# Reciprocal roots as a power on GpSimd, decay exponents in the bias of ScalarE's exponential, and one last convolution tap

## The chip, the core and the metric

The kernel runs on one core of a Trainium2 chip. The metric is device microseconds of one execution. The trace is one execution taken by the hardware profiler; its times are microseconds (us) unless marked ns. The five engines appear in it as PE (TensorE matmuls; PEld is its weight load), DVE (VectorE), ACT (ScalarE), POOL (GpSimd) and SP (SyncE, which only issues DMAs here). Each engine works through its own queue in order and waits for the others through semaphores.

## The reference

One inference step of a trunk of two layers, in float32, for a prompt of 512 tokens and 8 samples of one token that share the weights. Layer 0 mixes tokens by a gated MLP with spatial mixing in chunks of 128, layer 1 by a gated DeltaNet; each is followed by a SwiGLU part, and a norm ends the trunk. What bears on the change:

```python
def rmsnorm(x, g):
    xf = xf * lax.rsqrt(jnp.mean(xf * xf, axis=-1, keepdims=True) + EPS)

def l2norm(x):
    return xf * lax.rsqrt(jnp.sum(xf * xf, axis=-1, keepdims=True) + EPS)

# short convolution of 4 taps over q, k and v, samples from their own state
for j in range(1, CONV_W):
    y = y + full[:, j:j + T] * w[j]

# gated delta rule, in chunks
beta = jax.nn.sigmoid(b_raw)
gc = jnp.cumsum(g, axis=-1)
decay = jnp.where(incl, jnp.exp(gc_i - gc_j), 0.0)
L = jnp.where(strict, (k * beta) @ k.T * decay, 0.0)
Tm = inverse of (I + L)
A = (q @ k.T) * decay
```

The last block is shortened; the outputs are the activations of prompt and samples and the new states.

## The kernel before

The 520 columns (512 of the prompt, 8 of the samples) are kept features first and are worked in two halves of 256 and 264 columns. Each weight tile (128 output features, 512 KB) is loaded by SP's queue (L130), cast on ScalarE into a high part (L138) and subtracted into a low part (L139), on VectorE or, for some tiles, on GpSimd: in the delta layer the first 17 of the tiles in `order` (`POOL_LO`), and elsewhere the last two of an output projection. A half tile is then 24 matmuls, three per 128 input features (`products`, L168), so a tile is 48. `stream` splits a weight tile one ahead of its use. A scheduler orders each engine's instructions by the order of the program and by readiness; the transposes and norm matmuls inside `pin` keep their place among the matmuls. `after(n, step)` emits a step behind the n-th half tile from now.

**Roots.** `rsqrt` (L107 to L124) computes 1/sqrt by an integer guess and two polynomial steps: nine VectorE operations (L114 to L123) on 3 to 64 columns. It is called 34 times: ten times for the norms, eight for the keys, and for the spatial gate, the queries, the samples and the outputs of the scan. For a norm, TensorE sums squares over partitions (L205, L207), VectorE scales the sum (L208), `rsqrt` follows, VectorE puts the factor on a diagonal (L221), TensorE spreads it (L227), ScalarE copies it to SBUF (L230), and VectorE applies it to each product (L238).

**Keys.** The key stage is `key_tile` for eight heads. `conv_tile` (L568) multiplies two half products by the norm (L574), scales them by the first tap on ScalarE (L577), adds three taps on VectorE over 512 columns (L579) and a fourth operation for the eight columns of the samples (L580), and ends with a Silu on ScalarE (L581). Two half tiles later `normalise` transposes the key on TensorE (L618), squares it four times on ScalarE with an accumulated sum (L621), adds eps (L622), takes the root and scales on VectorE (L624). Four half tiles after the convolution `back` transposes again (L629). With the first four heads, `decay` loads rows by DMA, masks them on GpSimd (L558) and subtracts the cumulated decay on VectorE (L559); with heads 2 and 4 an Exp over 16 chunks at once follows on ScalarE (L654). `lower` multiplies key by key on TensorE (L643) and applies beta and decay in four VectorE operations per head (L645).

**Behind the keys.** The inverse of I + L is a chain of VectorE operations (L670 to L689) beside gate tiles; its blocks are merged with TensorE while `decay` and `query_conv` prepare the queries, with two more Exps of 16 chunks (L753). Then come the value tiles and the scan (`scan_step`), whose outputs take a root too (L832 to L836). The kernel ends with the last norm: L208, the root, then the scaling of the tokens out of PSUM (L1010 on ScalarE, L1012 on VectorE) and the stores.

Of the kernel before, what the change touches and what calls it, by code (L numbers as in the profile page):

```python
# [15 lines left out]
P = 128  # L16
# [22 lines left out]
def trunk(  # L39
# [55 lines left out]
    G.memset(ones, 1.0)  # L95
    warm = cst.tile([P, 1], F32, name="warm")
# [9 lines left out]
    # ---------------------------------------------------------------- helpers  # L106
    def rsqrt(s, n, p=P):  # L107
        if n <= 32:
            y = sm.tile([P, 32], F32, tag="rs_y", name=nm("rs_y"), bufs=4)[:p, :n]
            u = sm.tile([P, 32], F32, tag="rs_u", name=nm("rs_u"))[:p, :n]  # L110
        else:
            y, u = t1()[:p, :n], t1()[:p, :n]
        yi = y.bitcast(I32)
        V.tensor_scalar(yi, s.bitcast(I32), 1, None, ALU.logical_shift_right)  # L114
        V.tensor_scalar(yi, yi, -1, 0x5F1FFFF9, ALU.mult, ALU.add)
        # a Newton step with balanced error, scaled by 3/8, then one of third order
        V.scalar_tensor_tensor(u, y, -0.375 * 0.703952253, y, ALU.mult, ALU.mult)
        V.tensor_tensor(u, u, s, ALU.mult)  # L118
        V.scalar_tensor_tensor(y, u, 0.375 * 0.703952253 * 2.38924456, y, ALU.add, ALU.mult)
        V.scalar_tensor_tensor(u, y, 64.0 / 9.0, y, ALU.mult, ALU.mult)  # L120
        V.tensor_tensor(u, u, s, ALU.mult)
        V.scalar_tensor_tensor(u, u, -10.0 / 3.0, u, ALU.add, ALU.mult)
        V.scalar_tensor_tensor(y, u, 5.0, y, ALU.add, ALU.mult)  # L123
        return y  # L124
# [23 lines left out]
    def after(n, step):  # L148
        """Emit a step behind the n-th half tile of products from now."""
        steps.setdefault(done[0] + n, []).append(step)  # L150
# [26 lines left out]
    class Norm:  # L177
        """RMSNorm whose per-token factor is applied after the products."""
# [19 lines left out]
        def factors(self, h):  # L198
            c0, n = HALF[h]
            ps = axps()  # L200
            s = small([P, 3], "nrm_s")
            G.memset(s, 1.0)
            for i, (o, w) in enumerate(PARTS[h]):
                rest = self.rest.get(h)
                pin(PE.matmul(ps[:w, i:i + 1], lhsT=self.acc[:, c0 + o:c0 + o + w], rhs=ones[:, 0:1], start=True, stop=rest is None))  # L205
                if rest is not None:
                    pin(PE.matmul(ps[:w, i:i + 1], lhsT=rest[:, o:o + w], rhs=ones[:, 0:1], start=False, stop=True))  # L207
            V.tensor_scalar(s[:, 0:2], ps[:, 0:2], 1.0 / D, EPS, ALU.mult, ALU.add)  # L208
            if h:
                V.tensor_scalar(s[:NS, 2:3], ps[:NS, 2:3], 1.0 / D, EPS, ALU.mult, ALU.add)  # L210
            return rsqrt(s, 3)
# [29 lines left out]
    class Feed:  # L241
        """Takes finished tiles of x: parts of x * gain for the products, squares for the norm."""
# [43 lines left out]
    # the tensor engine's clock rises while the first loads run  # L286
# [4 lines left out]
    # ---------------------------------------------------------------- input  # L291
# [23 lines left out]
    # ---------------------------------------------------------------- layer 0: spatial gating  # L315
# [51 lines left out]
    V.tensor_scalar(sv, sv, 1.0 / DA, EPS, ALU.mult, ALU.add)  # L367
# [14 lines left out]
    V.tensor_scalar(svs, ps[:, :NS], 1.0 / DA, EPS, ALU.mult, ALU.add)  # L382
# [34 lines left out]
    # ---------------------------------------------------------------- swiglu  # L417
# [38 lines left out]
    # ---------------------------------------------------------------- layer 1: gated delta net  # L456
# [7 lines left out]
    # conv contributions of the sample states  # L464
# [28 lines left out]
    # beta and decay, columns in (head, chunk) order, the samples as a fifth chunk  # L493
# [26 lines left out]
    V.tensor_scalar(beta, beta, 1.0, None, ALU.add)  # L520
    V.reciprocal(beta, beta)
    V.scalar_tensor_tensor(sp, ax, 0.0, sp, ALU.max, ALU.add)
# [7 lines left out]
    V.tensor_copy(gc, ps[:, 0:32])  # L530
    egl = cst.tile([P, H, NCH], F32, name="egl")
# [12 lines left out]
    # samples: decay and the factors of the prediction  # L544
# [9 lines left out]
    # decay between the positions of a chunk, strictly lower: exp(gc_i - gc_j)  # L554
    def decay(t, hd, keep, sign, base):
        t4 = t[:, 4 * hd:4 * hd + 4]
        nc.sync.dma_start(t4, rows_v[0, hd].partition_broadcast(P))
        G.affine_select(t4, t4, [[0, 4], [-sign, C]], keep, sign * BIG, base=0, channel_multiplier=sign)  # L558
        V.tensor_tensor(t4, t4, gc[:, 4 * hd:4 * hd + 4, None].to_broadcast((P, 4, C)), ALU.subtract)  # L559
# [8 lines left out]
    def conv_tile(w, n, dst, y=None):  # L568
        raw = t2()
        V.memset(raw[:, 0:3], 0.0)  # L570
        for h in range(2):
            c0, nn = HALF[h]
            ps = mm3(w, KD, hb, h)
            V.tensor_tensor(raw[:, 3 + c0:3 + c0 + nn], ps[:, :nn], norm.r[:, c0:c0 + nn], ALU.mult)  # L574
        nc.sync.dma_start(cv_new[:, n, :], raw[:, 512:523])
        y = y if y is not None else t2()[:, :TT]
        S.activation(y[:, :T], raw[:, 0:T], AF.Copy, scale=wc[:, n, 0:1])  # L577
        for j in range(1, 4):
            V.scalar_tensor_tensor(y[:, :T], raw[:, j:j + T], wc[:, n, j:j + 1], y[:, :T], ALU.mult, ALU.add)  # L579
        V.scalar_tensor_tensor(y[:, T:TT], raw[:, 515:523], wc[:, n, 3:4], cs[:, n, :], ALU.mult, ALU.add)  # L580
        S.activation(dst if dst is not None else y, y, AF.Silu)  # L581
        return y
# [21 lines left out]
    # keys: normalise, decay  # L604
# [3 lines left out]
    def key_tile(hd):  # L608
# [5 lines left out]
        def normalise():  # L614
            pk = axps()
            ssk = small([P, NCH], "ssk")
            for c in range(NCH):
                pin(PE.transpose(pk[:, c * C:(c + 1) * C], kc[:, c * C:(c + 1) * C], ident))  # L618
            jk = t1()
            for c in range(NCH):  # L620
                S.activation(jk[:, :C], pk[:, c * C:(c + 1) * C], AF.Square, accum_out=ssk[:, c:c + 1])  # L621
            V.tensor_scalar(ssk, ssk, EPS, None, ALU.add)  # L622
            rk = rsqrt(ssk, 4)
            V.tensor_tensor(kn, lanes(pk), rk[:, :, None].to_broadcast((P, NCH, C)), ALU.mult)  # L624
# [13 lines left out]
    def lower(hd):  # L638
        q0 = hd * 4
        ps = axps()  # L640
        for c in range(NCH):
            kk = knT[:, hd, c * C:(c + 1) * C]
            PE.matmul(ps[:, c * C:(c + 1) * C], lhsT=kk, rhs=kk, start=True, stop=True)  # L643
        for c in range(NCH):
            V.scalar_tensor_tensor(L[:, q0 + c, :], ps[:, c * C:(c + 1) * C], beta[:, hd, c:c + 1], L[:, q0 + c, :], ALU.mult, ALU.mult)  # L645

    for hd in range(H):
# [4 lines left out]
        if hd in (2, 4):  # L652
            half = L[:, 8 * hd - 16:8 * hd]
            S.activation(half, half, AF.Exp, scale=-1.0)  # L654
# [6 lines left out]
    # inverse of I + L: 32 x 32 diagonal blocks by substitution, all at once  # L661
# [39 lines left out]
    # inverse: merge the blocks  # L701
# [47 lines left out]
    # queries: decay of the earlier positions, inclusive and transposed, then the products  # L749
    bv = region(3, [P, NCH, H, P], "bv")  # L750
    for gr in range(2):
        half = AT[:, 16 * gr:16 * gr + 16]
        S.activation(half, half, AF.Exp)  # L753
# [26 lines left out]
    # scan over the chunks, four heads at a time; the outputs take the place of the values  # L780
# [5 lines left out]
    def q_scale(gr):  # L786
        hs = slice(4 * gr, 4 * gr + 4)
        s16 = ssq[:, hs].rearrange("p h c -> p (h c)")
        r16 = rqs[:, hs].rearrange("p h c -> p (h c)")
        V.tensor_scalar(s16, s16, EPS, None, ALU.add)  # L790
        V.tensor_scalar(r16, rsqrt(s16, 16), float(P) ** -0.5, None, ALU.mult)
        V.tensor_tensor(rq2[:, hs], rqs[:, hs], rqs[:, hs], ALU.mult)

    def scan_step(gr, c):
# [37 lines left out]
        V.tensor_tensor(so, so, rq2[:, hs, c], ALU.mult)  # L832
        V.tensor_scalar(so, so, 1.0 / P, EPS, ALU.mult, ALU.add)
        ro = rsqrt(so, 4)
        V.tensor_tensor(ro, ro, rqs[:, hs, c], ALU.mult)
        (V if gr and c == 3 else G).tensor_tensor(o_c, o_c, ro[:, :, None].to_broadcast((P, 4, P)), ALU.mult)  # L836

    # samples: one step of the recurrence

    def sample_norm(gr):  # L840
# [7 lines left out]
        V.tensor_scalar(skq, ps[:, :64], EPS, None, ALU.add)  # L848
# [23 lines left out]
    def sample_finish(gr):  # L872
# [28 lines left out]
        V.tensor_scalar(so.rearrange("p (h b) -> p h b", h=4), total(kq), 1.0 / P, EPS, ALU.mult, ALU.add)  # L901
# [23 lines left out]
    # outputs: back to features, gain and gate  # L925
# [47 lines left out]
    # ---------------------------------------------------------------- second swiglu, final norm  # L973
    fin, xg = Norm(), []

    def last(k, h):
# [8 lines left out]
        if h:  # L985
            # scaled in place, features first
# [9 lines left out]
        else:  # L996
            # turned to tokens, scaled on the way out of PSUM
# [17 lines left out]
    # new states of the samples, between the products  # L1015
# [96 lines left out]
```

## Time and profile before

| | |
|---|---|
| median of three runs | 1501.97 us (1501.6 to 1502.32) |
| span of the profiled execution | 1499.8 us, 29605 instructions |
| lying outside the span, by the median | 2.2 us |
| TensorE busy | 1447.5 us (97%), 12192 matmuls |
| VectorE busy | 813.3 us (54%), 1727 instructions |
| ScalarE busy | 540.6 us (36%), 1067 instructions |
| GpSimd busy | 440.7 us (29%), 468 instructions |
| data moved by DMA | 155.69 MB, 104 GB/s in the mean |

The profiled execution's own time is given by its span, first to last instruction of the trace; what lies around it is the difference to the runs. A row of the timeline has the start and the duration of an instruction, its engine and line, the tiles written and read, and in brackets how long its engine stood idle before it and what released it. A row of the waits names the waiting line, the line waited for, the microseconds in total, the number of times and the longest. A group row has busy time, then the mean of one in ns, then the idle time before. PEclk is the granted clock of TensorE as a share of full speed.

### The profile page before, as it was taken

How to read it: one execution, taken by the hardware profiler on the slowest of the kernel's cores; microseconds unless marked ns; L12 is line 12 of the kernel's file. 1: busy time of each engine (PE TensorE's matmuls, PEld its weight loads, DVE VectorE, ACT ScalarE, POOL GpSimd, SP SyncE). 2: the span in 40 equal slices, each digit the busy share in tenths (PEclk: the TensorE clock that was granted, in tenths of full speed). 3: DMA queues.
4: the chain of work that ended last, by engine and by line, in shares of the span. 5: the costliest groups of instructions: out<-in, count | busy, mean ns of one | idle time of the engine just before them, and what ended most of it. 6: DMA issues, size and time to landing. Idle time of an engine off the chain costs nothing.

```text
span 1499.8 us, 29605 instructions
## 1 busy us (share of the span) xinstructions
PE 1447.5 (97%) x12192; PEld 1429.8 (95%) x12192; DVE 813.3 (54%) x1727; ACT 540.6 (36%) x1067; POOL 440.7 (29%) x468
## 2 busy tenths in 40 slices
PE   8999999999999999998788899999999999999997
PEld 8999999999999999998788888999999999999997
DVE  7447445553333333347777988686754344444344
ACT  5445323433312321334643255434433313321333
POOL 2113102333302320336444212311334412430333
PEclk9999999999999999999899999999999999999999
DMA  6222222322322232224311224234423443444331
GB/s 205 81 85 87 86 85 85 101 85 88 97 89 95 88 96 90 94 82 144 104 58 71 79 79 134 87 103 146 150 85 107 141 148 120 124 143 134 114 95 68
DMA packets 79367, 155.69 MB, mean 104 GB/s; under 512 B 10848, under 2 KB 41216, under 8 KB 79232
## 3 DMA queue, kind: packets, MB, share of 16 engines
q1 hardware_dynamic: 78944, 153.27, 31.1%
q8 instruction: 96, 1.57, 0.4%
q10 hardware_dynamic: 288, 0.52, 0.1%
q14 instruction: 39, 0.32, 0.1%
HBM read 142.18 MB, written 11.59 MB: 103 GB/s over the span
## 4 chain that ended last, share of the span: by engine, by line
PE 85%; DVE 11%; ACT 2%; issue 2%; DMA 1%; POOL 0%; SPq 0%; ACTq 0%; DVEq 0%; POOLq 0%
PE mm L168 76%; DVE kcs L579 1%; PE ax L406 1%; DVE sc L677 1%; DVE inv L678 1%; PE ax L867 1%; DVE t L579 1%; DVE sqacc L196 1%; PE ax L334 1%; DVE rs_u L118 1%; PE ax L643 1%; DVE inv L670 1%; PE sx L819 1%; PE sx L826 0%; PE ax L227 0%
## 5 line engine op out<-in xcount | busy, mean ns | idle before, releaser
L168 PE MATMUL mm<-hfh,wsp 128*128 128x256 f32 (+1 forms) x2816 | 510.4, 283 | 0.0
L168 PEld LDWEIGHTS mm<-hfh,wsp 128*128 128x128 f32 x2816 | 436.0, 189 | 0.1
L168 PE MATMUL mm<-hfl,wsp 128*128 128x256 f32 (+1 forms) x1408 | 398.8, 283 | 0.0
L138 ACT CAST wsp<-raw 128x1024 fp32r<-128x1024 f32 (+2 forms) x225 | 231.8, 1030 | 456.3 <-PE mm L168 408.5
L139 DVE TENSOR_TENSOR wsp<-raw,wsp 128x1024 fp32r<-128x1024 f32 (+2 forms) x193 | 234.0, 1213 | 91.4 <-ACT wsp L138 90.8
L168 PEld LDWEIGHTS mm<-hfl,wsp 128*128 128x128 f32 x1408 | 265.8, 189 | 0.0
L168 PE MATMUL mm<-fmh,wsp 128*128 128x264 f32 (+1 forms) x1408 | 254.9, 283 | 0.0
L168 PEld LDWEIGHTS mm<-fmh,wsp 128*128 128x128 f32 x1408 | 217.6, 188 | 0.0
L168 PE MATMUL mm<-hbh,wsp 128*128 128x264 f32 (+1 forms) x1024 | 203.9, 295 | 7.8 <-DVE t L574 5.7
L168 PE MATMUL mm<-hnh,wsp 128*128 128x264 f32 (+1 forms) x1024 | 197.9, 287 | 2.9 <-POOL wsp L139 1.0
L168 PE MATMUL mm<-fml,wsp 128*128 128x264 f32 (+1 forms) x704 | 198.9, 283 | 0.0
L430 POOL TENSOR_TENSOR t<-t,rbc 128x256 f32<-128x256 f32 x88 | 95.3, 1083 | 315.9 <-ACT t L429 315.9
L168 PEld LDWEIGHTS mm<-hbh,wsp 128*128 128x128 f32 x1024 | 166.8, 196 | 9.7 <-DVE t L574 6.3
L238 DVE TENSOR_TENSOR t<-mm,rbc 128x264 f32<-128x264 f32 (+1 forms) x160 | 68.4, 428 | 193.6 <-PE mm L168 192.1
L168 PEld LDWEIGHTS mm<-hnh,wsp 128*128 128x128 f32 x1024 | 161.5, 189 | 4.0 <-POOL wsp L139 1.2
L168 PE MATMUL mm<-hbl,wsp 128*128 128x264 f32 (+1 forms) x512 | 150.0, 293 | 0.0
L168 PE MATMUL mm<-hnl,wsp 128*128 128x256 f32 (+1 forms) x512 | 145.6, 285 | 0.4 <-DVE hnl L261 0.4
L175 POOL TENSOR_TENSOR fml<-t,fmh 128x256 fp32r<-128x256 f32 x88 | 95.9, 1089 | 150.0 <-ACT fmh L174 150.0
L168 PEld LDWEIGHTS mm<-fml,wsp 128*128 128x128 f32 x704 | 132.6, 188 | 0.0
L282 DVE TENSOR_TENSOR x<-mm,x 128x264 f32<-128x264 f32 (+1 forms) x128 | 54.5, 426 | 124.9 <-PE mm L168 124.5
L436 DVE TENSOR_TENSOR t<-mm,t 128x256 f32<-128x256 f32 x88 | 37.7, 429 | 119.2 <-PE mm L168 117.0
L168 PEld LDWEIGHTS mm<-hbl,wsp 128*128 128x128 f32 x512 | 100.3, 196 | 0.3
(331 smaller groups left out, 1989.9 us busy)
## 6 DMA issues: line engine op xcount, KB each, us to landing
raw<-in_f_w_in SPq DMA_DIRECT2D x88, 512.0 KB, 3.2
raw<-in_f_w_out SPq DMA_DIRECT2D x32, 512.0 KB, 3.5
raw<-in_b_w_in SPq DMA_DIRECT2D x32, 512.0 KB, 3.3
raw<-in_a_w_in SPq DMA_DIRECT2D x31, 512.0 KB, 3.2
raw<-in_a_w_out SPq DMA_DIRECT2D x16, 512.0 KB, 3.6
raw<-in_f_w_out SPq DMA_DIRECT2D x16, 384.0 KB, 3.1
L<-rows_d SPq DMA_DIRECT2D x16, 256.0 KB, 3.6
t<-in_st_delta SPq DMA_DIRECT2D x16, 256.0 KB, 3.2
```

The costliest lines, as they stand in the source:

```text
L118: V.tensor_tensor(u, u, s, ALU.mult)
L138: S.copy(hi, r)
L139: (eng or V).tensor_tensor(w[:, 1, i:i + n, :], r, hi.bitcast(F32), ALU.subtract)
L168: PE.matmul(ps[:, :n], lhsT=w[:, a, k, :], rhs=act[b][:, k, c0:c0 + n], start=(i == 0), stop=(i == last))
L175: (eng or G).tensor_tensor(act[1][:, k, c0:c0 + n], tmp, hi.bitcast(F32), ALU.subtract)
L196: (eng or G).tensor_tensor(a, a, t, ALU.add)
L238: V.tensor_tensor(t, ps[:, :n], self.r[:, c0:c0 + n], ALU.mult)
L282: V.tensor_tensor(dst, ps[:, :w], (xin(j)[:, c0:c0 + w] if xin else dst), ALU.add)
L334: PE.transpose(ps[:, j * P:(j + 1) * P], vf[j][:, c * C:(c + 1) * C], ident)
L430: G.tensor_tensor(s, s, norm.r[:, c0:c0 + nn], ALU.mult)
L436: V.tensor_tensor(sg[h], ps[:, :nn], sg[h], ALU.mult)
L579: V.scalar_tensor_tensor(y[:, :T], raw[:, j:j + T], wc[:, n, j:j + 1], y[:, :T], ALU.mult, ALU.add)
```

## The change

The nine operations of `rsqrt` become two on GpSimd: an addition of eps and a power with the exponent -0.5, read from a constant column. The callers no longer add eps: the two that did only that (L622, L790) go, and the others keep their scaling or a copy. The small multiplications by the query's root in the scan, and those of `q_scale`, move from VectorE to GpSimd. The subtraction of L559 goes: the cumulated decay enters as the bias of the Exp, one value per partition, so that each Exp over 16 chunks becomes 16 over one chunk. For the keys, beta is added to that bias as its logarithm, -Ln(1 + exp(-b)), bounded from below; `lower` is then one product over four chunks. The convolution's contribution of the samples' state is copied on ScalarE into the last 8 columns, and the last tap runs over 520 columns. The scratch space of DMA descriptors is given a size, and comments go, so that line numbers move. The core of the diff, with the place in the code instead of line numbers:

```diff
@@ constants @@
+    mhalf = cst.tile([P, 1], F32, name="mhalf")
+    G.memset(mhalf, -0.5)
@@ def rsqrt @@
-    def rsqrt(s, n, p=P):
...
-        yi = y.bitcast(I32)
-        V.tensor_scalar(yi, s.bitcast(I32), 1, None, ALU.logical_shift_right)
-        V.tensor_scalar(yi, yi, -1, 0x5F1FFFF9, ALU.mult, ALU.add)
...
-        V.scalar_tensor_tensor(u, y, -0.375 * 0.703952253, y, ALU.mult, ALU.mult)
-        V.tensor_tensor(u, u, s, ALU.mult)
-        V.scalar_tensor_tensor(y, u, 0.375 * 0.703952253 * 2.38924456, y, ALU.add, ALU.mult)
-        V.scalar_tensor_tensor(u, y, 64.0 / 9.0, y, ALU.mult, ALU.mult)
-        V.tensor_tensor(u, u, s, ALU.mult)
-        V.scalar_tensor_tensor(u, u, -10.0 / 3.0, u, ALU.add, ALU.mult)
-        V.scalar_tensor_tensor(y, u, 5.0, y, ALU.add, ALU.mult)
+    def rsqrt(s, n, p=P, eps=EPS):
+
+        y = sm.tile([P, 64], F32, tag="rs_y", name=nm("rs_y"), bufs=4)[:p, :n]
+        G.tensor_scalar(y, s, eps, None, ALU.add)
+        G.tensor_tensor(y, y, mhalf[:p].to_broadcast((p, n)), ALU.pow)
         return y
@@ Norm.factors @@
-            V.tensor_scalar(s[:, 0:2], ps[:, 0:2], 1.0 / D, EPS, ALU.mult, ALU.add)
+            V.tensor_scalar(s[:, 0:2], ps[:, 0:2], 1.0 / D, None, ALU.mult)
@@ beta and decay @@
     V.tensor_scalar(beta, beta, 1.0, None, ALU.add)
+    lnb = small([P, H, 5], "lnb")
+    S.activation(lnb, beta, AF.Ln)
     V.reciprocal(beta, beta)
+    V.tensor_scalar(lnb, lnb, -1.0, -BIG, ALU.mult, ALU.max)
...
+    gcb = cst.tile([P, 32], F32, name="gcb")
+    V.tensor_tensor(gcb.rearrange("p (h c) -> p h c", c=4), gc.rearrange("p (h c) -> p h c", c=4), lnb[:, :, 0:4], ALU.add)
+    ngc = cst.tile([P, 32], F32, name="ngc")
+    V.tensor_scalar(ngc, gc, -1.0, None, ALU.mult)
@@ def decay @@
         G.affine_select(t4, t4, [[0, 4], [-sign, C]], keep, sign * BIG, base=0, channel_multiplier=sign)
-        V.tensor_tensor(t4, t4, gc[:, 4 * hd:4 * hd + 4, None].to_broadcast((P, 4, C)), ALU.subtract)
+
+    def decay_exp(t, q0, sign, bias):
+        for q in range(q0, q0 + 16):
+            S.activation(t[:, q], t[:, q], AF.Exp, bias=bias[:, q:q + 1], scale=sign)
@@ def conv_tile @@
-        for j in range(1, 4):
-            V.scalar_tensor_tensor(y[:, :T], raw[:, j:j + T], wc[:, n, j:j + 1], y[:, :T], ALU.mult, ALU.add)
-        V.scalar_tensor_tensor(y[:, T:TT], raw[:, 515:523], wc[:, n, 3:4], cs[:, n, :], ALU.mult, ALU.add)
+        S.copy(y[:, T:TT], cs[:, n, :])
+        for j, m in ((1, T), (2, T), (3, TT)):
+            V.scalar_tensor_tensor(y[:, :m], raw[:, j:j + m], wc[:, n, j:j + 1], y[:, :m], ALU.mult, ALU.add)
@@ key_tile, normalise @@
-            V.tensor_scalar(ssk, ssk, EPS, None, ALU.add)
             rk = rsqrt(ssk, 4)
@@ def lower @@
-        for c in range(NCH):
-            V.scalar_tensor_tensor(L[:, q0 + c, :], ps[:, c * C:(c + 1) * C], beta[:, hd, c:c + 1], L[:, q0 + c, :], ALU.mult, ALU.mult)
+        V.tensor_tensor(L[:, q0:q0 + 4], lanes(ps), L[:, q0:q0 + 4], ALU.mult)
@@ the loop over the keys @@
         if hd in (2, 4):
-            half = L[:, 8 * hd - 16:8 * hd]
-            S.activation(half, half, AF.Exp, scale=-1.0)
+            decay_exp(L, 8 * hd - 16, -1.0, gcb)
@@ queries @@
-        half = AT[:, 16 * gr:16 * gr + 16]
-        S.activation(half, half, AF.Exp)
+        decay_exp(AT, 16 * gr, 1.0, ngc)
@@ q_scale @@
-        V.tensor_scalar(s16, s16, EPS, None, ALU.add)
-        V.tensor_scalar(r16, rsqrt(s16, 16), float(P) ** -0.5, None, ALU.mult)
-        V.tensor_tensor(rq2[:, hs], rqs[:, hs], rqs[:, hs], ALU.mult)
+        G.tensor_scalar(r16, rsqrt(s16, 16), float(P) ** -0.5, None, ALU.mult)
+        rp = small([P, 16], "rp")
+        G.tensor_scalar(rp, r16, 1.0 / P, None, ALU.mult)
+        G.tensor_tensor(rq2[:, hs].rearrange("p h c -> p (h c)"), rp, r16, ALU.mult)
@@ scan_step @@
-        V.tensor_tensor(so, so, rq2[:, hs, c], ALU.mult)
-        V.tensor_scalar(so, so, 1.0 / P, EPS, ALU.mult, ALU.add)
+        G.tensor_tensor(so, so, rq2[:, hs, c], ALU.mult)
         ro = rsqrt(so, 4)
-        V.tensor_tensor(ro, ro, rqs[:, hs, c], ALU.mult)
+        G.tensor_tensor(ro, ro, rqs[:, hs, c], ALU.mult)
@@ program @@
-    nc = _bacc.Bacc("TRN2", target_bir_lowering=False, num_devices=1)
+    nc = _bacc.Bacc("TRN2", target_bir_lowering=False, num_devices=1, dynamic_dma_scratch_size=64)
```

The remaining edits of the diff drop EPS in the same way from the factors of the spatial gate (L367, L382) and of the samples (L848, L901).

## Rows read from the trace of the kernel before

**Rows 1.** The page, part 4: the chain that ended last, by engine.

```profile
PE 85%; DVE 11%; ACT 2%; issue 2%; DMA 1%; POOL 0%; SPq 0%; ACTq 0%; DVEq 0%; POOLq 0%
```

**Rows 2.** TensorE's waits over the whole span; us in total, times, longest.

```profile
PE ax L629 <- DVE kns L624: 14.2, 4, 5.7
...
PE ax L227 <- DVE t L221: 8.3, 5, 2.3
...
PE mm L168 <- ACT wsp L138: 0.8, 1, 0.8
```

**Rows 3.** Two stretches: key stage, then inverse; busy us and instructions per engine.

```profile
714.00:816.00 102.00, 86.72 (x656) 84.33 (x657) 76.05 (x196) 52.71 (x122) 47.95 (x46) 0.91 0.24 80
...
816.00:874.00 58.00, 48.05 (x368) 46.90 (x367) 56.53 (x109) 17.98 (x20) 14.47 (x14) 0.91 0.22 74
```

**Rows 4.** Timeline around the key transposes at 748 us; start, duration, engine, line.

```profile
742.99 2.52 POOL L139 TENSOR_TENSOR wsp<-raw,wsp 128x1024 fp32r<-128x1024 f32 x1 [2.08 <-ACT wsp L138]
...
743.22 2.31 DVE L118 TENSOR_TENSOR rs_u<-rs_u,ssk 128x4 f32<-128x4 f32 x1
...
747.89 0.69 DVE L624 TENSOR_TENSOR kns<-ax,rs_y 128x512 f32<-128x512 f32 x1
...
748.64 0.90 PE L629 MATMUL ax<-ident,kns 128*128 128x128 f32 x3 [5.74 <-DVE kns L624]
```

**Rows 5.** Timeline before the norm of the second feed-forward part, around 1100 us.

```profile
1098.89 2.39 POOL L139 TENSOR_TENSOR wsp<-raw,wsp 128x1024 fp32r<-128x1024 f32 x1 [5.22 <-ACT wsp L138]
...
1098.91 2.39 DVE L118 TENSOR_TENSOR rs_u<-rs_u,nrm_s 128x3 f32<-128x3 f32 x1
...
1102.60 0.48 DVE L221 TENSOR_SCALAR t<-ident,rs_y 128x128 f32<-128x128 f32 x2
```

**Rows 6.** Timeline at the end of the kernel, VectorE.

```profile
1491.98 0.16 DVE L208 TENSOR_SCALAR nrm_s<-ax 128x2 f32<-128x2 f32 x1 [1.43 <-PE ax L207]
...
1493.95 0.75 DVE L1012 TENSOR_SCALAR t<-mm,rs_y 128x512 f32<-128x512 f32 x1
```

**Rows 7.** Stretches of 4 us, columns as in rows 3; after the bars, TensorE's clock.

```profile
748.00:752.00 4.00, 3.36 (x16) 3.37 (x17) 1.69 (x3) 2.02 (x8) 1.17 (x2) 0.50 0.05 12
...
752.00:756.00 4.00, 4.00 (x34) 4.00 (x33) 2.33 (x3) 1.46 (x5) 2.39 (x1) 0.95 0.02 4
...
1104.00:1108.00 4.00, 4.00 (x24) 4.00 (x22) 1.65 (x3) 0.85 (x3) 0.00 (x0) 0.57 0.41 138
```

**Rows 8.** GpSimd's groups by line and form, whole span; busy us, mean ns.

```profile
L377 POOL TENSOR_TENSOR t<-misc 128x128 f32<-128x128 f32 x1 | 0.4, 401 | 0.1
...
L412 POOL COPY t<-misc 128x8 f32<-128x8 f32 x16 | 3.1, 191 | 0.1
```

**Rows 9.** ScalarE's groups by line and form, whole span.

```profile
L621 ACT ACTIVATE t<-ax 128x128 f32<-128x128 f32 x32 | 8.8, 275 | 2.7 <-PE ax L618 2.2
...
L621 ACT ACTIVATION_READ_ACCUMULATOR t<-ax 128x1 f32 x32 | 6.3, 197 | 0.0
...
L654 ACT ACTIVATE L<-L 128x2048 f32<-128x2048 f32 x2 | 3.8, 1916 | 1.4 <-DVE L L559 1.4
...
L260 ACT ACTIVATE hfh<-x,gffn 128x256 fp32r<-128x256 f32 x16 | 8.1, 509 | 24.0 <-DVE x L282 24.0
...
L192 ACT ACTIVATE t<-x 128x256 f32<-128x256 f32 x35 | 13.8, 405 | 6.7 <-DVE x L282 6.7
...
L519 ACT ACT_TABLE_LOAD x1 | 1.3, 1283 | 0.0
...
L519 ACT ACTIVATE sp<-sp 128x40 f32<-128x40 f32 x1 | 0.2, 237 | 0.0
```

**Rows 10.** VectorE's groups by line, key stage, 714 to 816 us.

```profile
L579 DVE SCALAR_TENSOR_TENSOR kcs<-t,wc,kcs 128x512 f32<-128x512 f32 x24 | 24.2, 1010 | 1.6 <-ACT kcs L577 1.4
...
L645 DVE SCALAR_TENSOR_TENSOR L<-ax,beta,L 128x128 f32<-128x128 f32 x30 | 9.0, 344 | 10.7 <-PE ax L643 10.7
...
L559 DVE TENSOR_TENSOR L<-L,rows 128x512 f32<-128x512 f32 x8 | 6.7, 855 | 0.0
```

More of the change, by code (lines that the diff above doesn't have):

```diff
@@ L104, in const_load @@
         return t
-    def rsqrt(s, n, p=P):
[L108 to L112, printed above, removed]
-        yi = y.bitcast(I32)
-        V.tensor_scalar(yi, s.bitcast(I32), 1, None, ALU.logical_shift_right)
-        V.tensor_scalar(yi, yi, -1, 0x5F1FFFF9, ALU.mult, ALU.add)
-        V.scalar_tensor_tensor(u, y, -0.375 * 0.703952253, y, ALU.mult, ALU.mult)
-        V.tensor_tensor(u, u, s, ALU.mult)
-        V.scalar_tensor_tensor(y, u, 0.375 * 0.703952253 * 2.38924456, y, ALU.add, ALU.mult)
-        V.scalar_tensor_tensor(u, y, 64.0 / 9.0, y, ALU.mult, ALU.mult)
-        V.tensor_tensor(u, u, s, ALU.mult)
-        V.scalar_tensor_tensor(u, u, -10.0 / 3.0, u, ALU.add, ALU.mult)
-        V.scalar_tensor_tensor(y, u, 5.0, y, ALU.add, ALU.mult)
+    def rsqrt(s, n, p=P, eps=EPS):
+        y = sm.tile([P, 64], F32, tag="rs_y", name=nm("rs_y"), bufs=4)[:p, :n]
+        G.tensor_scalar(y, s, eps, None, ALU.add)
+        G.tensor_tensor(y, y, mhalf[:p].to_broadcast((p, n)), ALU.pow)
         return y
@@ L207, in factors @@
                     pin(PE.matmul(ps[:w, i:i + 1], lhsT=rest[:, o:o + w], rhs=ones[:, 0:1], start=False, stop=True))
-            V.tensor_scalar(s[:, 0:2], ps[:, 0:2], 1.0 / D, EPS, ALU.mult, ALU.add)
+            V.tensor_scalar(s[:, 0:2], ps[:, 0:2], 1.0 / D, None, ALU.mult)
             if h:
-                V.tensor_scalar(s[:NS, 2:3], ps[:NS, 2:3], 1.0 / D, EPS, ALU.mult, ALU.add)
+                V.tensor_scalar(s[:NS, 2:3], ps[:NS, 2:3], 1.0 / D, None, ALU.mult)
             return rsqrt(s, 3)
@@ L366, in trunk @@
     V.tensor_reduce(sv, ssv.rearrange("p u c -> p c u"), mybir.AxisListType.X, ALU.add)
-    V.tensor_scalar(sv, sv, 1.0 / DA, EPS, ALU.mult, ALU.add)
+    V.tensor_scalar(sv, sv, 1.0 / DA, None, ALU.mult)
     rv = rsqrt(sv, NCH)
@@ L381, in trunk @@
     PE.matmul(ps[:, :NS], lhsT=ones, rhs=svs, start=True, stop=True)
-    V.tensor_scalar(svs, ps[:, :NS], 1.0 / DA, EPS, ALU.mult, ALU.add)
+    V.tensor_scalar(svs, ps[:, :NS], 1.0 / DA, None, ALU.mult)
     rvs = rsqrt(svs, NS)
@@ L847, in sample_norm @@
         skq = small([P, 64], "skq")
-        V.tensor_scalar(skq, ps[:, :64], EPS, None, ALU.add)
+        V.tensor_copy(skq, ps[:, :64])
         r = rsqrt(skq, 64).rearrange("p (a h b) -> p a h b", a=2, h=4)
@@ L900, in sample_finish @@
         so = small([P, 32], "sso")
-        V.tensor_scalar(so.rearrange("p (h b) -> p h b", h=4), total(kq), 1.0 / P, EPS, ALU.mult, ALU.add)
+        V.tensor_scalar(so.rearrange("p (h b) -> p h b", h=4), total(kq), 1.0 / P, None, ALU.mult)
         ro = rsqrt(so, 32).rearrange("p (h b) -> p h b", h=4)
```

## The prediction

> **What bounds the kernel now.** I read the page first: TensorE carries 85% of the chain that ended last, VectorE 11% [rows 1]. So TensorE's matmuls set the time, and what can be won is the time in which it stands still because of a vector operation, and the slow clock behind such a stop. The list of TensorE's waits gives the first. Four waits of the key transposes (L629) for the normalised keys (L624) cost 14.2 us, five of the norm's spreading matmul (L227) for the scaled identity (L221) cost 8.3 us; a wait for a weight cast costs 0.8 us [rows 2]. The view by stretches places the keys' share: from 714 to 816 us TensorE is busy 86.72 of 102 us at a granted clock of 0.91, and the stretch behind it, 816 to 874 us with the inverse, is VectorE's own, busy 56.53 of 58 us [rows 3].
>
> The timeline of the longest key wait shows its cause. The reciprocal root (L114 to L123) is nine tiny VectorE operations; its L118, on 128x4 numbers, begins at 743.22 and lasts 2.31 us, while GpSimd's weight split (L139) runs for 2.52 us from 742.99. VectorE's queue is in order, conv taps slip in between, L624 begins only at 747.89, and TensorE has stood still for 5.74 us [rows 4]. At a norm it is the same: L118 takes 2.39 us beside a 2.39 us split, and L221 follows 3.69 us after L118 began [rows 5]. Where nothing disturbs, at the very end, the ten operations from L208 to just before L1012 take 1.97 us, 0.197 each [rows 6].
>
> After such a stop the clock is low: of the 4 us from 748 TensorE is busy 3.36, at a granted clock of 0.50, its lower level (1.2 GHz), with 16 matmuls; the next 4 us hold 34 at 0.95. From 1104, after the norm's gap, it makes 24 at 0.57 [rows 7].
>
> **The change, part by part.** The sum is made against the profiled span of 1499.8 us; the median of the runs is 1501.97, so 2.2 us are added at the end.
>
> *The root on GpSimd.* It becomes an addition of eps and a power. The power is nowhere in the trace. From below I bound it by GpSimd's 128x8 copy, 0.19 us [rows 8], from above by its large two-input operation, the split, 2.39 us [rows 5]. I take 0.40 us, the two-input operation on 128x128 [rows 8]: the operands here hold 3 to 64 columns, so that row is the nearest of its kind. With 0.19 for the addition and 0.06 per handoff (L624 ends at 748.58, L629's matmul begins at 748.64 [rows 4]) the root takes 0.7 us.
>
> *Norms.* Now, held, L208 to L221 takes 4 x 0.197 + 3.69 = 4.5 us; then it takes 0.2 + 0.7 = 0.9 us. That is 3.6 us earlier, against a mean wait of 1.7 (8.3 / 5), so all 8.3 go. A dip of the clock goes with them: 34 / 0.95 = 36 matmuls fit in 4 us, 9 per us; 24 ran, and the 12 missing are 1.3 us. Sum **-9.6**. With the power at its upper bound the root takes 2.7 us, and about 8 still go.
>
> *Keys.* Between normalise and transpose lies one weight tile of 48 matmuls, 48 / 9 = 5.3 us. The four squares with their accumulator reads take 4 x (0.275 + 0.197) = 1.9 us [rows 9], the root 0.7, a conv tap in front on VectorE up to 1.0 [rows 10], L624 itself 0.7 [rows 4]: 4.3 us, inside the tile. So the 14.2 us go, and the dips: 3.36 us at full clock hold 30 matmuls, 16 ran, 1.6 us after the longest stop; I take 1.3 for each of the four, 5.2. Gross 19.4.
>
> *Exponentials.* Against that stands ScalarE. Two Exps of 128x2048 (1.92 us) here, and two for the queries, become 16 each of 128x128. ScalarE's 128x128 row is 0.275; a pointer as scale adds 0.51 - 0.41 = 0.10 at 128x256, which I use for the bias: 0.28 to 0.38 each [rows 9]. At 0.33 a batch is 5.3 us, 3.4 longer. ScalarE is in order: behind a batch stand the weight cast that the next tile needs and the squares of the next key. I let both batches of this stage reach TensorE whole, with the same share of clock (5.2 / 14.2): 2 x 3.4 x 1.37 = 9.3. Keys net **-10.1**. For the two query batches, hidden by weights split ahead until that stock is gone, I put half of 2 x 3.4, **+3.4**.
>
> *Off VectorE, around the inverse.* The subtraction L559 (0.86 us, eight here, eight for the queries) goes; four beta products L645 of 0.34 become one from PSUM of 0.69, as L624; the sample tap L580 goes, and eight more columns in a last tap of 1.01 us cost nothing I can see [rows 4, 10]. Most of it lies beside matmuls. On the path is what starts the inverse later or lengthens it: the last two heads' L645, 2 x (4 x 0.34 - 0.69) = 1.3 less, of which I take **-1.0**, and one L559 or a few L580 inside its stretch, **-0.5**. The 24 ScalarE copies of the samples' part, at the 0.24 of a 128x40 row [rows 9], run while VectorE is still at the taps; without that cover they cost 6 us.
>
> *End.* L208 to L1012 falls from 1.97 to 0.9: **-1.0**.
>
> *Other roots* (q_scale, samples, scan) have no TensorE wait of size behind them [rows 2]. The new Ln of beta runs once, 0.24 us before the keys, beside TensorE's work. For the old Ln, L519, the trace has a table load of 1.28 us behind Exps [rows 9]; parted from it, the new one would cost two loads, 2.6 us, on the stage's way only if the decays wait for them. The Trainium skill ("ScalarE: Activation LUTs", Table sets) says that ln and exp share a set and need one load; by it the term is zero, by this trace up to 2.6 us; the measurement decides.
>
> Sum: -9.6 - 10.1 + 3.4 - 1.5 - 1.0 = -18.8; 1499.8 - 18.8 + 2.2 = 1483.2, say **1483 us**. With the power at 2.39 us each key comes 1 us late, 8 x 1.0 = 8, and the time is about 1493; if ScalarE's 12.7 us are hidden, 1470.
>
> **Rivals.** *A: the power is a long routine.* Nothing in the trace excludes more than 2.39 us. At 3 us a key's chain is 1.9 + 3.3 + 1.0 + 0.7 = 6.9 against 5.3, eight keys lose 13 where 19.4 were lost, ScalarE's 12.7 come on top, the norms gain only 5: no change. From there it decides. At 6 us norms come 2 us later than now on five waits (+10), keys lose 4.6 x 8 = 37 against 19.4 (+18), ScalarE 12.7, the end 5, less 1.5: 1502 + 44 = 1546. For it speaks only that the price is unknown; against it, three or four columns and rows of 0.19 and 0.40. Chance 0.16.
>
> *B: ScalarE becomes the bound of the key stage.* The sixteen Exps of a batch are ready apart; if Silus come between, each split of a batch costs two table loads, 2.6 us [rows 9]. With four splits: 1483 + 10 = 1493. For it: the queue is full of ready work. Against: ScalarE is busy 52.71 of 102 us, so 6.8 more need not bind [rows 3]. Chance 0.20, a tail of it (nine splits, 1506) slower.
>
> *C: moving work from VectorE to GpSimd gives nothing,* as both operations of a root stand behind a split of their own: 0.7 + 2 x 2.4 = 5.5 us against 4.5 for the held root. Then the norms gain nothing; if four of eight keys meet it, as now, each is 1.9 + 5.5 + 1.0 + 0.7 - 5.3 = 3.8 late, 15 against 19.4; with half of ScalarE's 12.7 and 2.5 of small gains, 1502 - 4 + 6 - 2 = 1502. The lock is in the trace [rows 4, 5], and GpSimd is busy 47.95 of 102 us in the key stage [rows 3]; against it, a split comes once per tile, not twice per root. Chance 0.10, on either side of no change. The Trainium skill ("Perfetto Trace Analysis", Optimizing Scalar/DVE Operations) warns that these two share a port, so that offloading between them might not help. The trace agrees on the port, with L118's 2.39 us; but what was held there is what this change takes off VectorE.
>
> **How the numbers follow.** The forecast case, 1470 to 1493, has 0.52; A 0.16, B 0.20, C 0.10; 0.02 is left for something slower that I don't see. The measurement can tell 0.2%, 3 us. Faster: 0.52 + 0.16 of B + 0.03 of C = 0.71. Within: 0.02 of B + 0.04 of C = 0.06. Slower: A, 0.02 of B, 0.03 of C and the rest, 0.23. The range 1470 to 1506 leaves out A and the rest.
>
> **What would show it.** Right: a power row near 0.4 us; the waits of the key transposes and of the norm's spreading matmul gone or below 1 us; the stretch from 714 shorter by 10 us with a clock above 0.95; 64 Exps near 0.33 us in four unbroken batches; about 1 us from the last L208 to the scaling. Wrong: a power above 3 us, more than two Exp table loads in the key stage, or TensorE waits for weight casts of several us.

## The result and the profile after

The changed kernel takes **1540.93 us** (median of 4 runs, 1539.6 to 1541.38) against 1502.14 us for the kernel before on the same chip: a ratio of 1.0249, with a 95% interval of 1.0226 to 1.0273. It is 39 us slower; 1483 us, faster, was forecast. The profiled span is 1539.6 us.

The page of the changed kernel, part 4, the chain that ended last by engine; GpSimd (POOL) had no share in it before [rows 1]:

```profile
PE 82%; DVE 6%; POOL 5%; ACT 3%; issue 2%; DMA 1%; SPq 0%; POOLq 0%; ACTq 0%; DVEq 0%
```

TensorE's waits in the changed kernel, columns as in [rows 2]:

```profile
PE ax L774 <- ACT t L582: 17.3, 4, 16.4
PE ax L864 <- issue: 10.6, 1, 10.6
PE ax L629 <- DVE kns L624: 6.4, 3, 2.6
PE ax L933 <- DVE t L934: 6.2, 1, 6.2
PE ax L217 <- DVE t L211: 5.5, 4, 3.2
```

The key transposes (L629) wait less than before, 6.4 us and another 2.7 behind L571 against 14.2, and so do the norms (L217), 5.5 against 8.3. The three long waits, L774, L864 and L933, are new; their longest single pieces make 33 us together, and none is at a key or a norm. L774 transposes the values, L864 is the samples' product, and L933 transposes the outputs of the scan. The list names no releaser for L864, but it waits 10.2 us too when only the two 64-column roots are powers (e4 below). GpSimd's groups by line and form point to the cause. L113 is the power:

```profile
L113 POOL TENSOR_TENSOR rs_y<-rs_y,mhalf 128x64 f32<-128x64 f32 x2 | 21.1, 10546 | 0.2
...
L113 POOL TENSOR_TENSOR rs_y<-rs_y,mhalf 128x4 f32<-128x4 f32 x17 | 18.1, 1066 | 1.2
...
L113 POOL TENSOR_TENSOR rs_y<-rs_y,mhalf 128x32 f32<-128x32 f32 x2 | 10.9, 5443 | 0.2
...
L113 POOL TENSOR_TENSOR rs_y<-rs_y,mhalf 128x3 f32<-128x3 f32 x10 | 8.8, 879 | 0.8
...
L113 POOL TENSOR_TENSOR rs_y<-rs_y,mhalf 128x16 f32<-128x16 f32 x2 | 6.8, 3425 | 0.1
```

A power costs by the column: 0.88 us at 3, 1.07 at 4, 3.43 at 16, 5.44 at 32 and 10.55 at 64 columns; from 32 to 64 it is 5.10 us for 32 columns, 0.16 each. The timeline of the longest wait shows how a long GpSimd operation reaches TensorE through two other queues:

```profile
1004.65 5.44 POOL L113 TENSOR_TENSOR rs_y<-rs_y,mhalf 128x32 f32<-128x32 f32 x1
...
1010.13 0.25 DVE L900 SCALAR_TENSOR_TENSOR pkq<-pkq,go,rs_y 128x32 f32<-128x32 f32 x1 [5.72 <-POOL rs_y L113]
...
1011.04 13.40 POOL L113 TENSOR_TENSOR rs_y<-rs_y,mhalf 128x64 f32<-128x64 f32 x2
...
1021.61 0.20 DVE L847 TENSOR_TENSOR kqs<-kqs,rs_y 128x32 f32<-128x32 f32 x1 [11.22 <-POOL rs_y L113]
...
1021.83 0.73 DVE L581 SCALAR_TENSOR_TENSOR t<-t,wc,t 128x512 f32<-128x512 f32 x1
...
1023.60 0.64 ACT L582 ACTIVATE t<-t 128x520 f32<-128x520 f32 x1 [20.48 <-DVE t L581]
...
1024.29 1.12 PE L774 MATMUL ax<-ident,t 128*128 128x128 f32 x4 [16.41 <-ACT t L582]
```

The row of 13.40 us joins two powers, of 64 and then of 16 columns; the first alone takes 10.54. VectorE reaches L900, which needs a 32-column power, and idles 5.72 us; then L847, which needs a 64-column one, and idles 11.22 us. The last convolution taps (L581) of a value tile stand behind both in VectorE's queue though they need neither. ScalarE's Silu (L582) waits 20.48 us for them, and TensorE 16.41 us for the Silu. The stretches below (columns as in [rows 3]) show TensorE at 70 matmuls in the 25 us around that wait, at a mean granted clock of 0.72, and the key stage where it was:

```profile
714.00:816.00 102.00, 86.90 (x668) 83.85 (x667) 56.92 (x83) 64.17 (x158) 59.28 (x66) 0.93 0.25 79
...
1000.00:1025.00 25.00, 8.59 (x70) 8.24 (x69) 6.30 (x18) 4.42 (x14) 22.08 (x9) 0.72 0.08 23
```

In the key stage VectorE lost 19 us of work (76.05 to 56.92) and ScalarE and GpSimd gained 11 each, but TensorE is busy for the same 87 us, with 668 matmuls against 656 [rows 3]: the relief bought next to nothing there.

### The profile page after: what moved, and what is told of

It reads as the page before. It is cut to its first block, busy times and chain, and to the rows that moved or that the text cites. A ratio compares the mean times of both kernels' runs of the same rounds, so it can differ in the third digit from the quotient of the medians.

```text
span 1539.6 us, 29392 instructions
## 1 busy us (share of the span) xinstructions
PE 1455.6 (95%) x12192; PEld 1436.5 (93%) x12192; DVE 747.3 (49%) x1322; ACT 563.6 (37%) x1160; POOL 520.6 (34%) x559
## 3 DMA queue, kind: packets, MB, share of 16 engines
q8 instruction: 96, 1.57, 0.4%
## 4 chain that ended last, share of the span: by engine, by line
PE 82%; DVE 6%; POOL 5%; ACT 3%; issue 2%; DMA 1%; SPq 0%; POOLq 0%; ACTq 0%; DVEq 0%
PE mm L158 74%; POOL rs_y L113 2%; POOL wsp L129 1%; DVE sc L675 1%; DVE t L581 1%; PE ax L864 1%; PE ax L396 1%; DVE inv L676 1%; PE sx L817 1%; PE ax L324 1%; DMA L<-rows_d 1%; PE sx L824 1%; ACT wsp L128 1%; DVE kcs L581 1%; POOL rs_y L112 0%
## 5 line engine op out<-in xcount | busy, mean ns | idle before, releaser
L158 PE MATMUL mm<-hbh,wsp 128*128 128x264 f32 (+1 forms) x1024 | 208.4, 298 | 12.2 <-DVE t L228 4.4
L158 PE MATMUL mm<-hbl,wsp 128*128 128x256 f32 (+1 forms) x512 | 151.3, 296 | 0.0
L158 PEld LDWEIGHTS mm<-hnl,wsp 128*128 128x128 f32 x512 | 96.6, 189 | 0.6 <-DVE hnl L251 0.6
```

Source lines behind the costliest of these rows:

```text
L158: PE.matmul(ps[:, :n], lhsT=w[:, a, k, :], rhs=act[b][:, k, c0:c0 + n], start=(i == 0), stop=(i == last))
```

## The experiments

All ratios are to the kernel before, run beside them on the same chip. The runs of one kernel spread by up to 6 us, those of the kernel before by up to 10 (1496.97 to 1507.4), so each ratio has its 95% interval beside it, and differences of 2 us or less are not read.

**The wide powers (e1 to e4).** The first run takes the roots of 8 and more columns back to VectorE:

```diff
+        if n <= 4:
...
+            G.tensor_scalar(y, s, eps, None, ALU.add)
+            G.tensor_tensor(y, y, mhalf[:p].to_broadcast((p, n)), ALU.pow)
+            return y
+        V.tensor_scalar(s, s, eps, None, ALU.add)
...
```

> The changed kernel with the roots of 8 and more columns (spatial-gate samples, q_scale, the samples' 32 and 64 columns) back as nine VectorE operations; only roots of 3 and 4 columns stay a power on GpSimd. Theory W (the power is priced per column, 10.5 us at 64, and the wide roots of the samples carry the loss): the 41.6 us that the changed kernel loses from 919 us on go, 1500 us, 1496 to 1505. Rival S (the 64 small Exps on ScalarE, or the small GpSimd operations of the scan, carry the loss): stays above 1515 us.

1501.86 us, ratio 0.9996 (0.9983 to 1.0008). Theory W holds: 39 us go with seven of the 34 roots, none of which serves a norm or a key.

The second has all roots as powers, and of the rest of the change only the scratch size (`rsqrt` is the one line `G.tensor_tensor(y, s, mhalf..., ALU.pow)`):

> The kernel before with every root a power on GpSimd and nothing else of the change but the size of the DMA scratch space, which makes room (eps stays with the callers). Theory W: nearly all of the loss is there, 1540 us, 1530 to 1548, with powers of about 0.16 us per column in the trace. Rival S: under 1510 us.

1532.69 us, 1.021 (1.019 to 1.023): the roots alone make 31 of the 39 us. The third has everything but the power (`rsqrt` is a VectorE addition and the nine operations):

> The changed kernel with all roots back as nine VectorE operations behind a VectorE addition of eps: what the Exps with bias, the shorter beta product, the last tap over 520 columns and the moved small products do alone. Theory W: about no change against before, 1496 to 1506 us. Rival S: above 1515 us.

1506.63 us, 1.0035 (1.0023 to 1.0047): 5 us, just above the range that was expected and far below that of rival S. Its roots are ten VectorE operations long, and the norm's spreading matmul waits 11.0 us in it. The fourth is the kernel before with only the two 64-column roots as powers:

> The kernel before with only the two roots of 64 columns as a power on GpSimd. Theory W: two powers of 10.5 us, each at the head of what the values' convolution on VectorE waits behind: 10.6 us at the first; at the second the 11.0 us of its own time; some 3 us of clock each: 1524 us, 1517 to 1532. Rival (each root costs a handoff, whatever its width): 1502 to 1505 us.

1525.17 us, 1.0158 (1.0134 to 1.0182). Its powers in GpSimd's groups:

```profile
L112 POOL TENSOR_TENSOR rs_p<-skq,mhalf 128x64 f32<-128x64 f32 x2 | 21.6, 10802 | 3.4 <-DVE skq L853 3.4
```

Two instructions cost 23.6 us, more than the 21.6 that they take. Two powers each of 16 and 32 columns, 17.7 us together, and one of 8 columns, 2.5 us, stand against the other 15 us of the 39; no run takes these alone.

**What the small powers gain (e5, e6).** The kernel before, plus:

```diff
+        if n <= 4:
+            y = sm.tile([P, 4], F32, tag="rs_p", name=nm("rs_p"), bufs=4)[:p, :n]
+            G.tensor_tensor(y, s, mhalf[:p].to_broadcast((p, n)), ALU.pow)
+            return y
```

> The kernel before with the roots of 3 and 4 columns as a power on GpSimd, all wider ones as before, nothing else of the change but the DMA scratch size. Theory W (only the wide powers lose): all roots as powers came to 1532.7 us, and from the 6528th to the 7296th weight matmul, where the wide ones lie, that kernel fell 40.0 us behind: 1493 us, 1490 to 1498. Rival T (the small roots gain nothing, since GpSimd's split then holds a conv tap where it held a root): 1500 to 1504 us.

1495.08 us, 0.9959 (0.9947 to 0.9971). For e6 the condition is `n == 3`, the norms alone:

> As the kernel with small powers only, but the 4-column roots (keys, scan, spatial gate) too stay on VectorE: only the ten norm factors are powers. Theory K (the gain lies at the norms, the keys' is lost again by the inverse): norms gain about 1.4 + 2.4 + 2.9 us: 1495 us, 1492 to 1499, no more than 2 us above the kernel with all small powers. Rival (the keys gain as forecast, 10 us): 5 us or more above that kernel.

1493.27 us, 0.9941 (0.9921 to 0.9961). Theory K holds: the norms alone give all of it, and the keys' powers add nothing that can be read. TensorE's waits of e6, keys and norms:

```profile
PE ax L634 <- DVE kns L629: 13.8, 4, 5.7
...
PE ax L232 <- DVE x L287: 2.7, 1, 2.7
...
PE ax L232 <- DVE t L226: 1.2, 2, 0.6
```

Of 8.3 us at the norms [rows 2] 3.9 are left, and 2.7 of these are laid on L287, not on a root. With the keys' powers (e5) the key transposes still wait 12.6 us, against 14.2 before:

```profile
PE ax L634 <- DVE kns L629: 12.6, 5, 4.5
```

**The Exps (e8, e9), the tap (e10).** To e5 are added the Exps with bias, the missing subtraction and the one beta product:

> The kernel with small powers only, with the Exps per chunk with bias, without L559's subtraction and with the one beta product, but without the 520-column tap and the moved small products. Theory X (the interrupted Exp batches cost some 6 us in key stage and inverse): 6 us above the kernel with small powers only, 1499 us, 1496 to 1503. Rival (the tap with its ScalarE copy, or the small products on GpSimd, cost it): within 2 us of the kernel with small powers only.

1495.19 us, 0.9958 (0.9943 to 0.9974), the same as e5. Theory X falls. The batches are indeed broken up, as ScalarE's groups of the changed kernel show, with eight table loads for all Exps of the decay where before there were four:

```profile
L560 ACT ACTIVATE L<-L,gcb 128x128 f32<-128x128 f32 x32 | 10.9, 398 | 0.1
L560 ACT ACT_TABLE_LOAD x8 | 10.3, 1283 | 0.1
```

But with VectorE relieved of the subtractions e8's key transposes wait 8.4 us where e5's wait 12.6, and 4.2 us of waits for weights split by GpSimd, against none in e5's list, take the place:

```profile
PE ax L645 <- DVE kns L640: 5.8, 3, 2.7
...
PE mm L173 <- POOL wsp L144: 4.2, 3, 1.8
...
PE ax L645 <- DVE t L586: 2.6, 1, 2.6
```

e9 holds ScalarE's Exps and Silus of e1 in program order (`pin(S.activation(...))`), with three Exp table loads left:

> The changed kernel with only 3- and 4-column powers (1501.9 us), whose per-chunk Exps and conv Silus on ScalarE are also held in the order of the program, so that a batch of sixteen is not broken up: 4 Exp table loads instead of 8, 10.3 us of ScalarE fewer. Theory X (the broken batches cost): 1496 us, 1493 to 1499. Rival (the longer batch itself, or the other edits): 1500 us or more, as behind a whole batch of 4.7 us the weight cast comes later.

1502.11 us, 1.0003 (0.999 to 1.0015): no gain from whole batches. In e10 only the tap of e1 is taken back:

> The changed kernel with only 3- and 4-column powers (1501.9 us), with the convolution's old taps: three over 512 columns and L580 for the samples, no ScalarE copy. It differs from the kernel with small powers and Exps (1495.2 us) only in the eps addition on GpSimd, the dropped eps operations and the scan's small products on GpSimd. Theory Y (the new tap with the ScalarE copy costs the 6.7 us between those two): 1496 us, 1493 to 1498. Rival Z (the second GpSimd operation per root and the moved products cost it): 1501 us, 1499 to 1504.

1500.84 us, 0.9995 (0.9981 to 1.0008): the tap costs nothing that can be read. What e10 has more than e8 is the eps addition on GpSimd and the small products.

**The second operation per root (e13).** To e5 is added

```diff
+            G.tensor_scalar(y, s, 0.0, None, ALU.add)
-            G.tensor_tensor(y, s, mhalf[:p].to_broadcast((p, n)), ALU.pow)
+            G.tensor_tensor(y, y, mhalf[:p].to_broadcast((p, n)), ALU.pow)
```

> The kernel with small powers only (1495.1 us), with an addition of zero on GpSimd ahead of each of these powers, as the change has one of eps; nothing else. Theory Z (the second GpSimd operation per root costs): 1499 us, 1497 to 1503. Rival (one more operation of 0.2 to 0.4 us is hidden): within 2 us of the kernel with small powers only.

1501.97 us, 0.9994 (0.9977 to 1.001), against 0.9959 without: about 5 us for 27 additions of 0.24 to 0.45 us (by the two intervals, 1 to 9). In its list of TensorE's waits the norms stand at 5.4 us against e5's 3.9 and the inverse's merge at 5.2 against 3.4; how the additions cost so much more than their place in the chain was not tested. With e8 and e10 showing no cost of the Exps and the tap, this is what leaves e1 no faster than before.

**Why the keys gained nothing (e11, e12, e14, e15).** In e5 the four squares ahead of the longest key wait lie 9.7 us apart, first to last, among an Exp and a Silu on ScalarE. e11 pins squares, Silus and Exps of e5 in program order, e12 those of e6:

> The kernel with small powers only (1495.1 us), whose key squares, conv Silus and key Exps on ScalarE keep the order of the program. In its trace the four squares of the key before the longest wait run from 728.4 to 738.1 us, between an Exp that waits for VectorE and a Silu. Theory Q (scattered squares, not the root, set the key transposes): the waits of the key transposes fall from 12.6 us to under 6, the time to 1489 us, 1485 to 1493. Rival V (VectorE's queue of subtractions and taps sets them): waits of 10 us or more, 1494 us or more.

> The same order on ScalarE, with powers only at the norms (1493.3 us without the order), the keys' roots on VectorE. Theory Q alone: the squares matter and the root does not, within 2 us of the kernel with ordered squares and small powers. If the key root counts once the squares are early: 4 us or more above that kernel, with key waits of 3 us or more left.

e11 1496.48 us, 0.9963 (0.9948 to 0.9978): the squares then lie within 2.7 us, the key waits are 11.6 us, and theory Q falls. e12 1502.57 us, 1.0006 (0.9995 to 1.0018), with key waits of 18.7 us. So with the order fixed the key root does count, 6 us between the two, as the second expectation of e12 has it; why the order itself costs e6 9 us stays open.

e14 leaves the key decays' subtraction out (so the keys' decay is not computed), with `scale=-0.001` in the Exp:

> The kernel with small powers only, without the eight subtractions of L559 in the key stage (the decay of the keys is left out, and the Exps there are scaled by 0.001 so that they stay finite). Theory V (VectorE's queue of subtractions and taps sets the key transposes): some 7 us of VectorE's work fewer, key waits under 7 us against 12.6, 1489 us, 1485 to 1492. Rival L (the lock with GpSimd's splits sets them): waits of 10 us or more, 1493 us or more.

1489.89 us, 0.9914 (0.9888 to 0.994), key waits 8.1 us: VectorE's load counts, in part. e15 is e5 with `POOL_LO = 0`, which moves the delta layer's weight splits from GpSimd to VectorE. They are 18, not 17: the first call of `stream` splits two tiles, and GpSimd has 28 splits of this size in e5 and 10 in e15:

> The kernel with small powers only, with all weight splits of the delta layer's input on VectorE, none on GpSimd there: VectorE gets 1.2 us per tile, 17 tiles, but is no longer held for 2.4 us by a split. Theory V: VectorE is the fuller for it, key waits of 12 us or more, 1496 us or more. Rival L: no VectorE operation of the key stage of over 2 us, key waits under 8 us, 1491 us or less.

**1480.10 us, 0.9849 (0.9823 to 0.9875).** Giving VectorE 18 splits more makes the kernel 15 us faster than e5. It is what rival L expects, and faster. In e5's timeline of the key stage, the two taps (the first row joins both) and the split beside them:

```profile
742.30 3.99 DVE L584 SCALAR_TENSOR_TENSOR kcs<-t,wc,kcs 128x512 f32<-128x512 f32 x2
742.91 2.83 POOL L144 TENSOR_TENSOR wsp<-raw,wsp 128x1024 fp32r<-128x1024 f32 x1
```

and the same taps in VectorE's groups of the key stage, 714 to 816 us, in e5:

```profile
L584 DVE SCALAR_TENSOR_TENSOR kcs<-t,wc,kcs 128x512 f32<-128x512 f32 x24 | 27.9, 1163 | 2.4 <-ACT kcs L582 2.1
```

and in e15, with the splits now VectorE's own (L144):

```profile
L584 DVE SCALAR_TENSOR_TENSOR kcs<-t,wc,kcs 128x512 f32<-128x512 f32 x24 | 18.3, 761 | 0.1
...
L144 DVE TENSOR_TENSOR wsp<-raw,wsp 128x1024 fp32r<-128x1024 f32 x13 | 17.4, 1341 | 2.2 <-ACT wsp L143 2.2
```

A tap takes 0.76 us alone, 1.01 in the kernel before [rows 10] and 1.16 in e5. Of the 24 key taps four run beside a split in the kernel before, at 1.85 us in the mean, and eight in e5, at 1.80; in e15 none does. So with the roots off VectorE the split more often finds a tap beside it instead of a 128x4 root operation, and holds that: this hold is the lock of the expectations. On GpSimd a split takes 2.4 us, on VectorE 1.3. The key transposes wait 6.6 us in e15, and another 1.6 for a weight cast:

```profile
PE ax L634 <- DVE kns L629: 6.6, 5, 3.7
...
PE ax L634 <- ACT wsp L143: 1.6, 1, 1.6
```

e15 also relieves GpSimd's queue and has each split done sooner, and no run parts this from the lock. The lists speak for the lock: summed over all rows, TensorE's waits for VectorE fall from 34.0 us in e5 to 23.6 in e15, while neither list has a wait for a split on GpSimd.

**The parts once the lock is gone (e16 to e19).** e16 is e6 with the Exps, still with splits on GpSimd:

> Powers only at the norms (1493.3 us), with the Exps per chunk with bias, without L559's subtraction and with the one beta product; key roots on VectorE. Theory: with VectorE relieved of subtractions and beta products, its key roots fit, and GpSimd carries no key powers: 1491 us, 1488 to 1495. Rival: as with small powers, what VectorE saves comes back as waits for casts and GpSimd's splits: within 2 us of 1493.

1494.71 us, 0.9944 (0.9925 to 0.9963): it lies in both ranges, and as e6 has 0.9941 the Exps gain nothing here, which is the rival. e17 is the kernel before with `POOL_LO = 0`, e18 is e8 and e19 is e1 with it:

> The kernel before, nothing of the change, with all weight splits of the delta layer's input on VectorE. If the lock alone is what the small powers met: the nine-operation roots are free of it too, and VectorE's extra work for them, some 1.2 us per key, is mostly hidden: 1485 us, 1480 to 1490. Rival (the power is needed to make room on VectorE for the splits): 1492 us or more.

> Small powers, Exps per chunk with bias, no L559, one beta product (1495.2 us), with all weight splits of the delta layer's input on VectorE. Theory: VectorE is the scarce queue of the stage once the lock is gone, and some 7 us less work there pays: 1475 us, 1471 to 1479. Rival (ScalarE's broken Exp batches bind instead): 1480 us or more.

> The changed kernel with only 3- and 4-column powers (1501.9 us), with all weight splits of the delta layer's input on VectorE. If the second GpSimd operation per root costs because it stands behind splits or under the lock: within 3 us of the kernel with small powers and Exps and the same splits. If it costs by itself: 5 us or more above that kernel.

e17 1483.82 us, 0.9873 (0.9847 to 0.99); **e18 1477.57 us, 0.9834 (0.9811 to 0.9856)**, the fastest kernel of the study; e19 1482.42 us, 0.9863 (0.9841 to 0.9886). Most of the gain is the splits' move alone; the small powers with the Exps are worth some 6 us on top (1483.82 to 1477.57, with intervals that just overlap). From e18 to e19 it is 4.8 us, between the two expectations, with overlapping intervals; e19 also has the new tap and the small products on GpSimd. Whether the second operation costs by itself or by what it stands behind stays open.

## Why the prediction was wrong

**The step that failed** is the price of the power: "I take 0.40 us, the two-input operation on 128x128 [rows 8]: the operands here hold 3 to 64 columns, so that row is the nearest of its kind". I priced an operation that no row shows by the shape of its operands, and one price for all widths. The power costs 0.16 us per column, 10.55 us at 64, above the 2.39 that I took as its bound from above: a bound taken from a subtraction says nothing of another function, as rival A half admitted ("Nothing in the trace excludes more than 2.39 us").

**The step that let it cost** is the one on the roots of q_scale, samples and scan, which "have no TensorE wait of size behind them". That was read from a list in which those roots took nine operations of 0.2 us. I did not ask what stood behind them in VectorE's queue: taps of a value tile. It cost 23.6 us by the two 64-column roots alone (e4), and 39 by all wide ones (e1).

**The power's price is not the whole miss.** Without the wide powers the changed kernel takes 1501.86 us (e1), no better than before, so the 18.8 us of forecast gain failed too: at the keys, and by the second operation of each root.

**Rival A** came near the time (1546 against 1541) for a wrong reason: it had a power of 6 us at every key and norm. At 3 and 4 columns the power is 0.9 to 1.1 us, under the 3 us from which that rival decides, and there the norms gained and the keys lost nothing. Its number was luck.

**Norms**: right for the power alone. -9.6 was forecast, and 1.0 for the end; e6, which has only these ten roots, the end's among them, gives 7.9 us by the medians (5.9 to 11.9 by its interval). But e6 has no addition on GpSimd: with it 5.4 us are waited at the norms (e13), and 5.5 in the changed kernel, where none was to be left.

**The end**: half of the forecast 1.0. In the timeline of the changed kernel L198 to the scaling takes 1.48 us, against 1.97 [rows 6], and GpSimd's two operations, from the first's start to the second's end, fill 1.20 of it:

```profile
1532.42 0.16 DVE L198 TENSOR_SCALAR nrm_s<-ax 128x2 f32<-128x2 f32 x1 [1.43 <-PE ax L197]
1532.67 0.23 POOL L112 TENSOR_SCALAR rs_y<-nrm_s 128x3 f32<-128x3 f32 x1 [0.29 <-DVE nrm_s L198]
1532.99 0.88 POOL L113 TENSOR_TENSOR rs_y<-rs_y,mhalf 128x3 f32<-128x3 f32 x1
1533.90 0.69 ACT L1007 ACTIVATE t<-mm,rs_y 128x512 f32<-128x512 f32 x1 [2.00 <-POOL rs_y L113]
1533.90 0.75 DVE L1009 TENSOR_SCALAR t<-mm,rs_y 128x512 f32<-128x512 f32 x1 [1.32 <-POOL rs_y L113]
```

**Keys**: wrong. "4.3 us, inside the tile. So the 14.2 us go" was to be the largest term; 12.6 us stayed (e5), and 9.1 in the changed kernel, where VectorE is also rid of the subtractions. The 4.3 us added durations as if each step found its engine free. The wait was laid on the root because the lock stood at L118; the lock belongs to the split, and the next VectorE operation takes it over (the taps of e5, against those of e15). Rival C had this lock but as a delay of GpSimd's operations. The Trainium skill ("Perfetto Trace Analysis", Optimizing Scalar/DVE Operations) warned that offloading between these two engines might not help; I set it aside since "what was held there is what this change takes off VectorE". The trace agrees with the page for the keys, by a tap of 1.16 us against 0.76, and not for the norms.

**Exponentials**: the broken batches of rival B came (eight Exp table loads for four, in the key stage five for two), but ScalarE did not become the bound: +9.3 and +3.4 were forecast, e8 shows no net cost with the lighter VectorE in it, and whole batches (e9) gain nothing. One Exp takes 0.40 us, above the 0.28 to 0.38 taken, but they overlap: five in a row take 1.57 us. The new Ln came right behind the old one and needed no load of its own; that term was zero because the two share a load, for a table is still loaded at the old Ln (L509) and again at the Exp behind it (L544), 1.28 us each, as before.

**Second operation**: priced at 0.19 us inside a root that was covered; it takes 0.23 us at a norm and 0.39 at a key, and 27 of them cost some 5 us (e13), a term that the sum did not have.

## What to carry to other kernels

Price an operation that no row shows by what it computes, not by its shape; allow for a price per column, and ask what a wide instance would hold up. When a wait is put down to an operation that runs far longer than its kind, ask what held it: taking the victim away leaves the holder, and the next one in the queue is held. A result that comes late to an in-order queue delays all that stands behind it, whether it needs it or not.

## What was not expected of the hardware

A power of two operands on GpSimd takes 0.16 us per column of 128 partitions, where a 128x16 multiplication on the same engine takes 0.22 us in all. GpSimd's weight split holds VectorE's taps as it held the roots' small operations: moving 18 splits of 2.4 us to VectorE, where they take 1.3, shortened the kernel by 17 us even with nothing of the change (e17). And 27 GpSimd additions of under half a microsecond cost about 5 us; why so much stays open.
